# Stepping the RWKV recurrence by halves of two neighbouring pairs, with the centring products beside the steps

## The chip, the cores and the metric

The kernel runs on one core of one Trainium2 chip, alone. The metric is the device time of one launch in microseconds, the median of three runs.

## The reference

Two layers over 512 tokens and 2048 channels. Layer A is RWKV-7 time mixing: four 2048x2048 projections (receptance, keys, values, gates), two low-rank paths, a recurrence over time for 32 heads of 64 channels, an output projection and a LayerNorm. Layer B is differential attention over 8 heads with its own projections, an output projection and a LayerNorm. What the change touches is the recurrence:

```python
def step(S, inp):
    r_t, w_t, k_t, v_t, kk_t, a_t = inp
    sa = jnp.einsum('bhvk,bhk->bhv', S, kk_t)
    S = (S * w_t[:, :, None, :]
         - sa[..., None] * (kk_t * a_t)[:, :, None, :]
         + v_t[..., None] * k_t[:, :, None, :])
    y = jnp.einsum('bhvk,bhk->bhv', S, r_t)
    return S, y
...
mu = jnp.mean(y, -1, keepdims=True)
yc = y - mu
var = jnp.mean(yc * yc, -1, keepdims=True)
y = (yc * lax.rsqrt(var + GN_EPS)).reshape(B, T, C) * gn_g + gn_b
```

The kernel does it by chunks of 64 tokens: within a chunk everything is products with a prepared inverse, and only the state goes from chunk to chunk.

## The kernel before

**Dense products.** Each projection is 16 products (one per 128 output channels, 512 tokens wide). A product is 16 steps, and a step is three 128x512 matmuls into the PSUM tile `mm` (operands are split in two parts: `xh,whi`, then `xl,whi`, then `xh,wlo`). After each step `product` calls `fill.tick()`. A tick lets each waiting job (a Python generator) trace its next piece; `yield n` makes a job sit out n ticks. So between the three matmuls of one step and those of the next there is one place, called a **gap** below, where other matmuls can stand, and TensorE (`mm` keeps its program order) runs them there. A gap with nothing in it is a bare one.

**Pairs.** Two heads of 64 channels make a pair, 16 pairs in all. `phase1` prepares the operands of a pair during the key products and stores them in DRAM; `solve` (GpSimd) and `join` invert the triangular systems, still partly during the value products. From the third value product on, `phase2(p)` loads a pair again and makes its matrices, `chain(p)` steps through its 8 chunks, and `post(p)` normalises, in gaps of the value products and then of the gate products.

- `phase2(p)`, by fours of chunks: `K` times `AR` (128x128 products, `big<-AR,bdK`), masked by DVE into `LAR`; the **centring products** (`big<-cst,vt`, 16 of 128x64) whose result ACT copies into `W`; transposes of `K` (`big<-cst,bdK`); `X` times `R` (`big<-R,bdX`), copied into `Q` (`qs`). Loads: `R`, `AR` and `K` (`bdK`) come ahead (`load_r`, `load_ar`, `load_k`); `load_x` loads `bz`, `gls` and `X` (`bdX`). All these DMAs stand in one queue, SP's, in program order.
- `chain(p)`, per chunk: in one gap the two products `u<-W,LAR` (one per head, 128x64); ACT copies them into `W` (L829, L830); GpSimd makes `nl`, the decayed state (L836). In the next gap two products `u<-W,qs`, from which DVE makes the next chunk's state (L844, `W<-u,gls,nl`), and four products `y<-...` (128x64) for the output. So a chunk takes two gaps, a pair 16, and the pairs follow each other.
- `post(p)`: square, sum over a head (two 128x512 products, `onesr`), a reciprocal root on DVE, and the store `d_y`. `gates` loads `d_y` again, after gate product `GL`, when the recurrence's memory is given back.

TensorE gets 64-column products from `u`, `y` and the centring alone; the products of `K`, `X` and the transposes have 128 columns, like the dense ones. A call of one product of these small ones appears in the trace as two records.

Of the kernel before, what the change touches and what calls it, by code (L numbers as in the profile page):

```python
# [36 lines left out]
WL = 3                 # half blocks of weights in flight  # L37
# [6 lines left out]
# columns of the table of constants  # L44
# [4 lines left out]
# per-channel vectors, [128, NT] each  # L49
# [25 lines left out]
class Fill:  # L75
    """Jobs (generators) traced in steps between the dense products; a job yields the number of steps to sit out."""
# [22 lines left out]
def trunk(ctx, tc, xT, wts, vecs, wa1, wa2, lamb, subg, consts, outT):  # L99
# [44 lines left out]
    paired = [i * NT for i in (0, 1, 2, 3, 5, 9)]     # blocks multiplied together with the next one  # L144
    QT = 4                                              # k-tiles per split
# [57 lines left out]
    def products(xparts, n, begin, end, make=None, after=None):  # L203
        """n products; the first two, when paired, take turns so that each x part is needed less soon."""
# [30 lines left out]
    def rsqrt(src, pool, shape, tag, bufs=2, act=False):  # L235
        """q with RS_C * q = src ** -0.5: a seed from the exponent, then Newton's and Halley's steps."""
# [75 lines left out]
    # A transposed and the inverse X by 32 x 32 blocks: upper rows of A, its lower right block, X11, X21 and X22  # L312
# [19 lines left out]
    # ================= layer 1: RWKV-7 =================  # L332
# [19 lines left out]
    idle = p0.tile([P, T], F32, name="idle")      # products that only bring the tensor engine up to its clock  # L352
# [19 lines left out]
    def mm3(ps, a, b, start=True, stop=True):  # L372
        """Product of operands in two parts each."""
# [105 lines left out]
    def decay(p):  # L479
        """What pair p needs besides its keys."""  # L480
# [31 lines left out]
    def phase1(p, ks):  # L512
# [7 lines left out]
        # 1 / |kk| per head and token  # L520
# [94 lines left out]
    def join(g):  # L615
# [6 lines left out]
        def diagonal(dst, src):  # L622
            """The blocks of each two systems, on the diagonal."""
# [56 lines left out]
    def open_p2():  # L680
# [33 lines left out]
    def load_x(p):  # L714
# [3 lines left out]
        bz = p2.tile([P, T], F32, tag="bz", name="bz", bufs=1)  # L718
        gls = p2.tile([P, NCH], F32, tag="gls", name="gls", bufs=3)
        dma(bz, d_kz[p][:, T:2 * T])  # L720
# [6 lines left out]
        sts[p].update(bz=bz, gls=gls)  # L727
# [6 lines left out]
    def phase2(p):  # L734
        yield from until(("v", p), ("ar", p))
        if p >= 2:
            yield from until(("chain", p - 2))
        (R, AR), vt = lds.pop(p), vts.pop(p)
        st = sts[p] = {}
        fill.add(load_x(p), 1)  # L740
        K, X, Q = fixed["K"], fixed["X"], fixed[p % 2]
        LAR = p2.tile([P, 2, 2, NCH, L], F32, tag="LAR", name="LAR")
        W = p2.tile([P, 2, NCH, 2, L], F32, tag="W", name="W")
        for h, r in HEADS:
            dma(LAR[r, h], AR[r].rearrange("p w (c t) -> p w c t", t=L))
        G.memset(W[lo_, 0, 0, 0], 0.0)
        G.memset(W[hi_, 1, 0, 0], 0.0)
        more = p + 1 < NPAIR
        if more:
            fill.add(load_r(p + 1), 1)  # L750
        for q in range(2):
            cq = slice(q * 4, q * 4 + 4)
            pk = big()
            for i in range(4):
                c = q * 4 + i
                mm(pk[:, i * P:(i + 1) * P], lhsT=K[:, c, :], rhs=AR[:, :, c * L:(c + 1) * L], start=True, stop=True)
                if i == 1:
                    yield 1
            pkv = pk.rearrange("p (c two t) -> p c two t", two=2, t=L)
            for h, r in ((0, hi_), (1, lo_)):  # L760
                for w, msk in ((0, m_lt), (1, m_le)):
                    V.tensor_tensor(LAR[r, h, w, cq], pkv[r, :, w], over(msk[r], [L, 4, L]), ALU.mult)
            yield 1
        if more:
            fill.add(load_ar(p + 1), 9)
        # centred v by tokens
        pt = big()
        for c in range(NCH):
            cs = slice(c * L, (c + 1) * L)
            for h, r in ((0, hi_), (1, lo_)):  # L770
                mm(pt[r, cs], lhsT=vt[:, cs], rhs=cen[:, h * L:(h + 1) * L], start=True, stop=True)
            if c % 4 == 3:
                cq = slice(c - 3, c + 1)
                ptv = pt.rearrange("p (c o t) -> p c o t", t=L, o=1)[:, cq]
                S.copy(W[hi_, 0, cq], ptv[hi_].broadcast_to([L, 4, 2, L]))
                S.copy(W[lo_, 1, cq], ptv[lo_].broadcast_to([L, 4, 2, L]))
                yield 1
        for q in range(2):
            cq = slice(q * 4, q * 4 + 4)
            pt = big()  # L780
            for i in range(4):
                transpose(pt[:, i * P:(i + 1) * P], K[:, q * 4 + i, :], ident)
            ptv = pt.rearrange("p (c t) -> p c t", t=P)
            S.copy(Q[hi_, 0, cq, 0:L], ptv[hi_, :, 0:L])
            S.copy(Q[lo_, 1, cq, 0:L], ptv[lo_, :, L:P])
            yield 2
        if more:
            fill.add(load_k(p + 1), 3)
        yield from until(("ldx", p))
        for q in range(2):  # L790
            cq = slice(q * 4, q * 4 + 4)
            px = big()
            for i in range(4):
                c = q * 4 + i
                mm(px[:, i * P:(i + 1) * P], lhsT=X[:, c, :], rhs=R[:, c].rearrange("p a t -> p (a t)"), start=True, stop=True)
                if i == 1:
                    yield 1
            pxv = px.rearrange("p (c t) -> p c t", t=P)
            S.mul(Q[lo_, 0, cq], pxv[lo_], -1.0)
            S.mul(Q[hi_, 1, cq], pxv[hi_], -1.0)  # L800
            yield 1
        # bonus
        bv = p2.tile([P, T], F32, tag="bv", name="bv")
        V.tensor_mul(bv, vt, st["bz"])
        st.update(W=W, Q=Q, bv=bv, LAR=LAR)
        yield 1
        done.add(("p2", p))

    def phases2():
        yield 8  # L810
        for p in range(NPAIR):
            yield from phase2(p)

    def chains():
        for p in range(NPAIR):
            yield from until(("p2", p))
            yield from chain(p)
            fill.add(post(p), 1)

    def chain(p):  # L820
        st = sts[p]
        W, LAR, Q, gls = st["W"], st["LAR"], st["Q"], st["gls"]
        py = ps_y.tile([P, T], F32, tag="y", name="y")
        for c in range(NCH):
            pu = ps_u.tile([P, T], F32, tag="u", name="u")
            for h, r in HEADS:
                mm(pu[r, 0:L], lhsT=LAR[:, h, 0, c], rhs=W[:, h, c, 0], start=True, stop=True)
            with tc.high_priority():
                S.copy(W[lo_, 0, c, 1], pu[lo_, 0:L])  # L829
                S.copy(W[hi_, 1, c, 1], pu[hi_, 0:L])  # L830
            cs = slice(c * L, (c + 1) * L)
            gl = gls[:, c:c + 1]
            if c + 1 < NCH:
                nl = p2.tile([P, L], F32, tag="nl", name="nl")
# [475 lines left out]
```

## Time and profile before

| | us |
|---|---|
| runs | 2369.32, 2369.45, 2372.07; median 2369.45 |
| profiled execution, span from first to last instruction | 2371.4 |
| TensorE busy in it | 2281.1 (96%) |
| VectorE, ScalarE, GpSimd busy | 1371.7, 1085.0, 598.1 |
| mean granted TensorE clock | 0.983 |

The profiled execution has no time of its own beside its span; the span lies inside the range of the three runs and 1.95 us above their median. TensorE is the engine to look at. Its busy time is not its work, though: matmuls overlap, so a stretch in which each starts later than it could still counts as busy. What a gap costs is read from the starts of the matmuls in order of time.

### The profile page before, as it was taken

The numbers are of one execution on the slowest core, as the hardware profiler recorded it, in microseconds if no ns is written. First come the engines' busy times: TensorE is split into PE (matmuls) and PEld (weight loads), VectorE is DVE, ScalarE is ACT, GpSimd is POOL, SyncE is SP. The second block draws the span as 40 slices with busy tenths as digits, with TensorE's granted clock in tenths as the row PEclk, the third lists the DMA queues.
The fourth block names the chain that finished last, engine by engine and source line by source line (L and its number), as shares of the span: only waits on it lengthen the run. The fifth ranks groups of instructions, "written<-read, shape, count | busy, mean of one in ns | idle before, by whom it ended". The sixth has DMA issues, their size and how long they took to land.

```text
span 2371.4 us, 34536 instructions
## 1 busy us (share of the span) xinstructions
PE 2281.1 (96%) x12894; PEld 1822.3 (77%) x12894; DVE 1371.7 (58%) x2451; ACT 1085.0 (46%) x2228; POOL 598.1 (25%) x817
## 2 busy tenths in 40 slices
PE   8999999989999999999999989999999999999995
PEld 5887877777667776678888768888888888888884
DVE  7556887795566666764445465353453544536554
ACT  6556655564555556643333353343333433334223
POOL 4223052858563335720023240000000000000113
PEclk9999999989999999999999999999999999999997
DMA  6445555577546545533333312222222222222222
GB/s 213 143 136 178 169 190 177 170 222 213 135 126 162 150 132 146 153 102 135 116 107 120 116 62 89 89 80 89 89 81 96 80 91 81 89 89 80 98 90 88
DMA packets 195079, 294.93 MB, mean 124 GB/s; under 512 B 115296, under 2 KB 119648, under 8 KB 194912
## 3 DMA queue, kind: packets, MB, share of 16 engines
q10 hardware_dynamic: 45648, 166.22, 20.8%
q1 hardware_dynamic: 144144, 109.71, 16.3%
q0 software_dynamic: 5120, 16.81, 2.5%
q8 instruction: 101, 1.65, 0.3%
q14 instruction: 66, 0.54, 0.1%
HBM read 239.13 MB, written 45.15 MB: 120 GB/s over the span
## 4 chain that ended last, share of the span: by engine, by line
PE 79%; POOL 7%; DVE 4%; issue 3%; DMA 3%; ACT 2%; SPq 1%; POOLq 0%; ACTq 0%; DVEq 0%
PE mm L105 64%; PE big L105 6%; PE u L105 2%; POOL z L605 2%; POOL tm L603 2%; DMA xin<-in_xT 2%; PE s L105 1%; PE y L105 1%; PE o L105 1%; PE big L108 1%; POOL xm L269 1%; SPq L111 1%; PE t L108 1%; POOL xin L268 1%; DVE wlo L176 1%
## 5 line engine op out<-in xcount | busy, mean ns | idle before, releaser
L105 PE MATMUL mm<-xh,whi 128*128 128x512 f32 x2560 | 1043.6, 408 | 6.7 <-ACT xh L231 2.3
L105 PE MATMUL mm<-xl,whi 128*128 128x512 f32 x2560 | 1006.7, 393 | 11.5 <-DVE xl L232 6.6
L105 PE MATMUL mm<-xh,wlo 128*128 128x512 f32 x2560 | 1006.3, 393 | 5.7 <-DVE wlo L176 5.5
L176 DVE TENSOR_TENSOR wlo<-wraw,whi 128x512 fp32r<-128x512 f32 x640 | 474.5, 742 | 597.7 <-ACT whi L175 564.3
L175 ACT CAST whi<-wraw 128x512 fp32r<-128x512 f32 x640 | 396.9, 620 | 727.3 <-PE mm L105 712.7
L105 PEld LDWEIGHTS mm<-xh,wlo 128*128 128x128 f32 x2560 | 483.9, 189 | 112.3 <-DVE wlo L176 8.5
L105 PEld LDWEIGHTS mm<-xl,whi 128*128 128x128 f32 x2560 | 485.4, 190 | 105.2 <-DVE xl L232 10.6
L105 PEld LDWEIGHTS mm<-xh,whi 128*128 128x128 f32 x2560 | 484.7, 189 | 104.6 <-ACT xh L287 4.9
L1118 POOL TENSOR_SCALAR dist<-dist 128x512 f32<-128x512 f32 x8 | 12.4, 1546 | 654.6 <-DVE zz L1148 654.6
L836 POOL TENSOR_SCALAR nl<-W,gls 64x64 f32<-64x64 f32 x224 | 115.0, 513 | 158.6 <-DVE W L844 146.3
L844 DVE SCALAR_TENSOR_TENSOR W<-u,gls,nl 64x64 f32<-64x64 f32 x224 | 63.4, 283 | 91.8 <-PE u L105 70.5
L266 ACT ACTIVATE xm<-xin,omu 128x512 f32<-128x512 f32 x96 | 68.2, 721 | 46.3 <-DMA xin<-in_xT 36.8
L603 POOL TENSOR_TENSOR tm<-z,at 128x31 f32<-128x31 f32 (+15 forms) x124 | 81.1, 654 | 31.1 <-DMA at<-d_ad 22.8
L605 POOL TENSOR_TENSOR z<-z,tm 128x31 f32<-128x31 f32 (+15 forms) x124 | 85.9, 693 | 8.4
L969 POOL TENSOR_TENSOR lna<-lna,zt 128x512 f32<-128x512 f32 x26 | 42.6, 1639 | 170.0 <-DVE zt L1244 115.8
L268 POOL TENSOR_SCALAR xin<-xin,vec 128x512 f32<-128x512 f32 x54 | 48.7, 902 | 140.6 <-ACT xm L266 52.1
L269 POOL TENSOR_TENSOR xm<-xm,xin 128x512 f32<-128x512 f32 x54 | 81.8, 1517 | 3.5
L829 ACT COPY W<-u 64x64 f32<-64x64 f32 x128 | 26.3, 205 | 101.6 <-PE u L105 94.7
L105 PEld LDWEIGHTS u<-W,LAR 128*64 128x64 f32 x512 | 28.7, 135 | 55.5 <-DVE W L844 27.3
L1077 POOL TENSOR_TENSOR xin<-xin,lns 128x512 f32<-128x512 f32 x15 | 19.7, 1311 | 194.6 <-ACT lns L957 148.9
L1147 ACT ACTIVATE sc<-sc,mx 128x128 f32<-128x128 f32 (+3 forms) x64 | 35.9, 561 | 57.8 <-DVE mx L1145 57.8
L288 DVE TENSOR_TENSOR xl<-xm,xh 128x512 fp32r<-128x512 f32 x64 | 57.4, 909 | 6.4 <-ACT xh L287 5.6
(246 smaller groups left out, 2742.2 us busy)
## 6 DMA issues: line engine op xcount, KB each, us to landing
wraw<-in_w_in ACTq DMA_DIRECT2D x125, 512.0 KB, 3.7
wraw<-in_w_oa ACTq DMA_DIRECT2D x32, 512.0 KB, 3.6
wraw<-in_w_v ACTq DMA_DIRECT2D x32, 512.0 KB, 3.5
wraw<-in_w_k ACTq DMA_DIRECT2D x32, 512.0 KB, 3.4
wraw<-in_w_q ACTq DMA_DIRECT2D x32, 512.0 KB, 3.5
wraw<-in_w_g ACTq DMA_DIRECT2D x32, 512.0 KB, 3.5
wraw<-in_w_ob ACTq DMA_DIRECT2D x32, 512.0 KB, 3.5
xin<-in_xT POOLq DMA_DIRECT2D x48, 256.5 KB, 3.8
```

The lines of the kernel that those rows point to most:

```text
L105: tc.keep_in_program_order(nc.tensor.matmul(*args, **kw))
L108: tc.keep_in_program_order(nc.tensor.transpose(*args))
L175: S.copy(hi, raw)
L176: V.tensor_sub(lo, raw, hi.bitcast(F32))
L266: S.mul(t, xt[:, 1:T + 1], sc)
L268: G.tensor_scalar(xp, xp, mu, 0.0, ALU.mult, ALU.add)
L269: G.tensor_add(t, t, xp)
L288: V.tensor_sub(lo, raw, hi.bitcast(F32))
L603: G.tensor_tensor(tv, z[:, j:j + 1, 0:n].broadcast_to([P, ni, n]), at_[:, j, j + 1:H2].rearrange("p (i o) -> p i o", o=1).broadcast_to([P, ...
L605: G.tensor_tensor(z[:, j + 1:H2, 0:n], z[:, j + 1:H2, 0:n], tv, ALU.subtract)
L836: G.tensor_scalar(nl[r], W[r, h, c, 0], gl[r], 0.0, ALU.mult, ALU.add)
L844: V.scalar_tensor_tensor(W[r, h, c + 1, 0], pm_[r, 0:L], gl[r], nl[r], ALU.mult, ALU.add)
```

## The change

A pair's preparation is cut in two: `phase2(p)` becomes `half(p, 0)` and `half(p, 1)`, each for four chunks, with `LAR`, `W` and `Q` of half the size and four of each in place of two. A round of `chain` now steps two halves together: chunk i of `half(p, 0)` and chunk i of `half(p - 1, 1)`, in the same PSUM tile. Its first gap has four products `u<-W,LAR`, its second four `u<-W,qs` and eight `y`; between them `yield 2` leaves a gap out. There are 17 rounds of 4 chunks, 4 gaps each, in place of 16 of 8 chunks with 2. The centring products are not traced where `half` comes to them, but put in the list `cols`, and `run_cols` places them right ahead of the next `u` products. `load_ar` and `load_k` come later in a pair and `load_x` earlier relative to their use; `bz` is gone, its data is loaded into `bv`. The output is copied to `ys` by halves and squared from there. `GL` is 5.

```diff
-        for i in range(2):
-            fixed[i] = p2.tile([P, 2, NCH, P], F32, name=f"qs{i}", bufs=1)
+        for i in range(4):
+            fixed[i] = p2.tile([P, 2, HC, P], F32, name=f"qs{i}", bufs=1)
...
-        dma(bz, d_kz[p][:, T:2 * T])
...
+    HC = NCH // 2
+    cols = []
+    going = [False]
+
+    def run_cols():
+        while cols:
+            cols.pop(0)()
+
+    def half(p, q):
+
+        if q == 0:
+            yield from until(("v", p), ("ar", p))
+            sts[p] = dict(zip(("R", "AR"), lds.pop(p)), vt=vts.pop(p))
+            fill.add(load_x(p), 1)
+            if p + 1 < NPAIR:
+                fill.add(load_r(p + 1), 1)
...
+        n = 2 * p + q
+        if n >= 4:
+            yield from until(("ch", n - 4))
+        K, X, Q = fixed["K"], fixed["X"], fixed[n % 4]
+        LAR = p2.tile([P, 2, 2, HC, L], F32, tag="LAR", name="LAR", bufs=4)
+        W = p2.tile([P, 2, HC, 2, L], F32, tag="W", name="W", bufs=4)
...
+            dma(LAR[r, h], AR[r].rearrange("p w (c t) -> p w c t", t=L)[:, :, cq])
...
+        if q:
+
+            if p >= 3:
+                yield from until(("y", p - 3))
+            st["bv"] = p2.tile([P, T], F32, tag="bv", name="bv", bufs=3)
+            dma(st["bv"], d_kz[p][:, T:2 * T])
...
+        if q and p + 1 < NPAIR:
+            fill.add(load_ar(p + 1), 2)
+        yield 1
+
+        def centred():
+
+            pt = big()
+            for i in range(HC):
+                cs = slice((q * HC + i) * L, (q * HC + i + 1) * L)
+                for h, r in ((0, hi_), (1, lo_)):
+                    mm(pt[r, i * L:(i + 1) * L], lhsT=vt[:, cs], rhs=cen[:, h * L:(h + 1) * L], start=True, stop=True)
+            ptv = pt[:, 0:HC * L].rearrange("p (c o t) -> p c o t", t=L, o=1)
+            S.copy(W[hi_, 0], ptv[hi_].broadcast_to([L, HC, 2, L]))
+            S.copy(W[lo_, 1, :, 1], ptv[lo_, :, 0])
+            S.copy(W[lo_, 1, :, 0], ptv[lo_, :, 0])
+            done.add(("cen", p, q))
+
+        cols.append(centred)
...
+        if q and p + 1 < NPAIR:
+            fill.add(load_k(p + 1), 1)
+        yield 2
+        yield from until(("ldx", p))
...
+        if q:
+            V.tensor_mul(st["bv"], vt, st["bv"])
+            done.add(("vt", p))
...
+        for s in range(NPAIR + 1):
+            act = [(s - 1, 1)] * (s > 0) + [(s, 0)] * (s < NPAIR)
+            for p, q in act:
+                yield from until(("p2", p, q))
+            going[0] = True
+            yield from chain(act)
+            going[0] = False
+
+    def chain(act):
+        py = ps_y.tile([P, 2, HC * L], F32, tag="y", name="y")
+        for i in range(HC):
+            run_cols()
             pu = ps_u.tile([P, T], F32, tag="u", name="u")
...
+            for e, (p, q) in enumerate(act):
+                W, LAR, Q = sts[p][q]
+                for h, r in HEADS:
+                    mm(pu[r, e * L:(e + 1) * L], lhsT=LAR[:, h, 0, i], rhs=W[:, h, i, 0], start=True, stop=True)
...
+            yield 2
+            if i + 1 == HC and act[-1][1] == 0:
+                yield from until(("w", act[-1][0], 1))
+            run_cols()
+            pm_ = ps_u.tile([P, T], F32, tag="u", name="u")
...
-    GL = 4
+    GL = 5
```

**TensorE, a value product in the middle of the recurrence, before.** Every gap holds a step's products, and each is followed by the three dense ones:

```order
L105 MATMUL u<-W,LAR 64x64 x2
L105 MATMUL big<-AR,bdK 128x128 x2
L105 MATMUL mm<-xh,whi 128x512
L105 MATMUL mm<-xl,whi 128x512
L105 MATMUL mm<-xh,wlo 128x512
L105 MATMUL u<-W,qs_5827 64x64 x2
L105 MATMUL y<-LAR,W 64x64
L105 MATMUL y<-qs_5827,W 64x64
L105 MATMUL y<-LAR,W 64x64
L105 MATMUL y<-qs_5827,W 64x64
L105 MATMUL big<-AR,bdK 128x128 x2
```

The same place after, from the first gap of a product to the third:

```order
L105 MATMUL u<-W,LAR 64x64 x4
L105 MATMUL big<-AR,bdK 128x128 x2
L105 MATMUL mm<-xh,whi 128x512
L105 MATMUL mm<-xl,whi 128x512
L105 MATMUL mm<-xh,wlo 128x512
L105 MATMUL big<-AR,bdK 128x128 x2
L105 MATMUL mm<-xh,whi 128x512
L105 MATMUL mm<-xl,whi 128x512
L105 MATMUL mm<-xh,wlo 128x512
L105 MATMUL u<-W,qs_5827 64x64 x2
L105 MATMUL u<-W,qs_5829 64x64 x2
L105 MATMUL y<-LAR,W 64x64
```

The `u` products of two halves stand together now, and the gap between two steps of the recurrence holds 128-column products alone.

**VectorE, the same product, before:** the state (`W<-u,gls,nl`) of a step stands ahead of the masks (`LAR<-big,cst`).

```order
L804 TENSOR_TENSOR bv<-vt,bz 128x512
L176 TENSOR_TENSOR wlo<-wraw,whi 128x512
L864 TENSOR_TENSOR lo<-y_9259,hi 128x512
L844 SCALAR_TENSOR_TENSOR W<-u,gls,nl 64x64 x2
L762 TENSOR_TENSOR LAR<-big,cst 64x256 x4
L844 SCALAR_TENSOR_TENSOR W<-u,gls,nl 64x64 x2
```

After:

```order
L176 TENSOR_TENSOR wlo<-wraw,whi 128x512
L906 TENSOR_TENSOR lo<-y_9469,hi 128x512
L823 TENSOR_TENSOR bv<-vt,bv 128x512
L779 TENSOR_TENSOR LAR<-big,cst 64x256 x4
L878 SCALAR_TENSOR_TENSOR W<-u,gls,nl 64x64 x4
L176 TENSOR_TENSOR wlo<-wraw,whi 128x512
```

The multiplication by `bv`, whose operand is loaded in the same product now, and the masks stand between two states.

**SP's queue, one pair, before** (the rows of `join` between `R` and `AR` in some pairs are not in this one):

```order
L111 DMA LAR<-AR 64x1024 x2
L111 DMA bz<-d_kz_128 128x512
L111 DMA gls<-d_kz_128 128x8
L111 DMA bdX<-d_xu_162 32x8x32
L111 DMA bdX<-d_xl_166 32x8x64
L111 DMA bdX<-d_xu_162 32x8x32
L111 DMA bdX<-d_xl_166 32x8x64
L111 DMA R<-d_rb_145 128x1024
L111 DMA AR<-d_ar_113 128x1024
L111 DMA bdK<-d_kz_129 64x8x64 x2
```

After, from the second half of a pair on:

```order
L111 DMA LAR<-AR 64x2x256 x2
L111 DMA bv<-d_kz_128 128x512
L111 DMA AR<-d_ar_113 128x1024
L111 DMA bdK<-d_kz_129 64x8x64 x2
L111 DMA LAR<-AR 64x2x256 x2
L111 DMA gls<-d_kz_129 128x8
L111 DMA bdX<-d_xu_162 32x8x32
L111 DMA bdX<-d_xl_166 32x8x64
L111 DMA bdX<-d_xu_162 32x8x32
L111 DMA bdX<-d_xl_166 32x8x64
L111 DMA R<-d_rb_146 128x1024
```

The next pair's `AR` follows the copy of the second half at once, and its `LAR` copies and `X` loads follow that `AR`.

## Rows read from the trace of the kernel before

**Rows 1.** Page: span; busy time and share of TensorE.

```profile
span 2371.4 us, 34536 instructions
...
PE 2281.1 (96%) x12894; PEld 1822.3 (77%) x12894; DVE 1371.7 (58%) x2451; ACT 1085.0 (46%) x2228; POOL 598.1 (25%) x817
```

**Rows 2.** Stretches: length; busy of PE, PEld, DVE, ACT, POOL; PEclk, DMA share, GB/s.

```profile
720.90:913.70 192.80, 192.63 (x1916) 137.90 (x1914) 118.83 (x259) 109.62 (x279) 60.99 (x125) 1.00 0.56 148
913.70:1007.10 93.40, 84.65 (x739) 59.29 (x738) 73.43 (x128) 63.01 (x147) 69.97 (x93) 0.98 0.55 147
```

**Rows 3.** TensorE in order of time (start, duration): a bare gap between.

```profile
1100.06 0.39 PE L105 MATMUL mm<-xh,wlo 128*128 128x512 f32 x1
...
1100.73 0.39 PE L105 MATMUL mm<-xh,wlo 128*128 128x512 f32 x1
```

**Rows 4.** TensorE in order of time: two `u` products in one gap.

```profile
759.97 0.40 PE L105 MATMUL mm<-xh,wlo 128*128 128x512 f32 x1
760.30 0.34 PE L105 MATMUL u<-W,LAR 128*64 128x64 f32 x4
...
761.13 0.40 PE L105 MATMUL mm<-xh,wlo 128*128 128x512 f32 x1
```

**Rows 5.** TensorE in order of time: eight centring products in one gap.

```profile
574.26 0.40 PE L105 MATMUL mm<-xh,wlo 128*128 128x512 f32 x1
...
575.78 0.40 PE L105 MATMUL mm<-xh,wlo 128*128 128x512 f32 x1
```

**Rows 6.** TensorE in order of time: four `y` products in one gap.

```profile
788.80 0.40 PE L105 MATMUL mm<-xh,wlo 128*128 128x512 f32 x1
...
790.08 0.40 PE L105 MATMUL mm<-xh,wlo 128*128 128x512 f32 x1
```

**Rows 7.** TensorE in order of time: two `u` and four `y` products.

```profile
776.23 0.40 PE L105 MATMUL mm<-xh,wlo 128*128 128x512 f32 x1
...
777.67 0.40 PE L105 MATMUL mm<-xh,wlo 128*128 128x512 f32 x1
```

**Rows 8.** TensorE in order of time: two `u` and eight centring products.

```profile
770.58 0.40 PE L105 MATMUL mm<-xh,wlo 128*128 128x512 f32 x1
...
772.20 0.40 PE L105 MATMUL mm<-xh,wlo 128*128 128x512 f32 x1
```

**Rows 9.** TensorE in order of time: two `K` times `AR` products alone.

```profile
569.70 0.39 PE L105 MATMUL mm<-xh,wlo 128*128 128x512 f32 x1
...
570.84 0.39 PE L105 MATMUL mm<-xh,wlo 128*128 128x512 f32 x1
```

**Rows 10.** TensorE in order of time: two `u`, two `X` times `R`.

```profile
780.66 0.40 PE L105 MATMUL mm<-xh,wlo 128*128 128x512 f32 x1
...
782.26 0.40 PE L105 MATMUL mm<-xh,wlo 128*128 128x512 f32 x1
```

**Rows 11.** SP's queue in order of time, at the first pair.

```profile
570.49 1.15 SPq L111 DMA_DIRECT2D LAR<-AR  x2
...
575.08 0.45 SPq L111 DMA_DIRECT2D bdX<-d_xl  x1
```

**Rows 12.** Tile `bdX`, 690 to 900 us: from issue to landing.

```profile
DMA to landing us min/median/max: 2.0/2.5/6.1
```

**Rows 13.** Tile `bz`, 690 to 900 us: from issue to landing.

```profile
DMA to landing us min/median/max: 2.9/4.0/5.0
```

**Rows 14.** VectorE, 720.9 to 913.7 us: busy, mean ns, idle before.

```profile
L844 DVE SCALAR_TENSOR_TENSOR W<-u,gls,nl 64x64 f32<-64x64 f32 x98 | 27.8, 283 | 38.8 <-PE u L105 37.0
L762 DVE TENSOR_TENSOR LAR<-big,cst 64x256 f32<-64x256 f32 x56 | 21.2, 418 | 1.2 <-PE big L105 0.5
...
L804 DVE TENSOR_TENSOR bv<-vt,bz 128x512 f32<-128x512 f32 x7 | 4.8, 692 | 10.6 <-DMA d_y<-bv 10.5 <-DVE W L844 0.2
```

**Rows 15.** DMA issues, 720.9 to 913.7 us: KB each, median us to landing.

```profile
LAR<-AR SPq DMA_DIRECT2D x14, 256.0 KB, 3.9
...
AR<-d_ar SPq DMA_DIRECT2D x7, 512.0 KB, 4.7
```

More of the change, by code (lines that the diff above doesn't have):

```diff
@@ L726, in load_x @@
             dma(X[m_:(h + 1) * L, :, h * L:(h + 1) * L], d_xl[g][s0:s0 + NCH].rearrange("c i e -> i c e"))
-        sts[p].update(bz=bz, gls=gls)
+        sts[p].update(gls=gls)
         done.add(("ldx", p))
@@ L732, in start_loads @@
             fill.add(f(p), delay)
[L734 to L743, printed above, removed]
-        for h, r in HEADS:
[L745 to L762, printed above, removed]
-            yield 1
[L764 to L807, printed above, removed]
@@ L810, in phases2, with halves2 @@
+    def halves2():
         yield 8
         for p in range(NPAIR):
-            yield from phase2(p)
+            for q in range(2):
+                yield from half(p, q)
     def chains():
[L815 to L824, printed above, removed]
+        for s in range(NPAIR + 1):
[5 more added lines that the diff above has]
+            going[0] = False
@@ L825, in chain @@
+    def chain(act):
+        py = ps_y.tile([P, 2, HC * L], F32, tag="y", name="y")
+        for i in range(HC):
+            run_cols()
             pu = ps_u.tile([P, T], F32, tag="u", name="u")
-            for h, r in HEADS:
-                mm(pu[r, 0:L], lhsT=LAR[:, h, 0, c], rhs=W[:, h, c, 0], start=True, stop=True)
+            for e, (p, q) in enumerate(act):
+                W, LAR, Q = sts[p][q]
+                for h, r in HEADS:
+                    mm(pu[r, e * L:(e + 1) * L], lhsT=LAR[:, h, 0, i], rhs=W[:, h, i, 0], start=True, stop=True)
@@ L828, in chain @@
             with tc.high_priority():
[L829 to L834, printed above, removed]
-                for h, r in HEADS:
-                    G.tensor_scalar(nl[r], W[r, h, c, 0], gl[r], 0.0, ALU.mult, ALU.add)
-            yield 1
-            if c + 1 < NCH:
-                pm_ = ps_u.tile([P, T], F32, tag="u", name="u")
-                for h, r in HEADS:
-                    mm(pm_[r, 0:L], lhsT=Q[:, h, c, 0:L], rhs=W[:, h, c, 1], start=True, stop=True)
-                with tc.high_priority():
-                    for h, r in HEADS:
-                        V.scalar_tensor_tensor(W[r, h, c + 1, 0], pm_[r, 0:L], gl[r], nl[r], ALU.mult, ALU.add)
@@ L845, in chain @@
-            for h, r in HEADS:
-                mm(py[r, cs], lhsT=W[:, h, c, 0], rhs=LAR[:, h, 1, c], start=True, stop=False)
-                mm(py[r, cs], lhsT=W[:, h, c, 1], rhs=Q[:, h, c, L:P], start=False, stop=True)
-            yield 1
-        ys = p2.tile([P, T], F32, tag="ys", name="ys", bufs=1)
-        S.copy(ys, py)
-        st["ys"] = ys
-        y2 = p2.tile([P, T], F32, tag="y2", name="y2", bufs=1)
-        S.activation(y2, py, AF.Square)
-        st["y2"] = y2
-        done.add(("chain", p))
+                for e, (p, q) in enumerate(act):
+                    W = sts[p][q][0]
+                    for h, r in HEADS:
+                        S.copy(W[r, h, i, 1], pu[r, e * L:(e + 1) * L])
@@ new lines, in chain @@
+            nls = {}
+            go_on = [(e, p, q) for e, (p, q) in enumerate(act) if q == 0 or i + 1 < HC]
+            for e, p, q in go_on:
+                W, gl = sts[p][q][0], sts[p]["gls"][:, q * HC + i:q * HC + i + 1]
+                nl = nls[e] = p2.tile([P, L], F32, tag=f"nl{e}", name="nl", bufs=1)
+                for h, r in HEADS:
+                    G.tensor_scalar(nl[r], W[r, h, i, 0], gl[r], 0.0, ALU.mult, ALU.add)
+            yield 2
+            if i + 1 == HC and act[-1][1] == 0:
+                yield from until(("w", act[-1][0], 1))
@@ new lines, in chain @@
+            run_cols()
+            pm_ = ps_u.tile([P, T], F32, tag="u", name="u")
+            for e, p, q in go_on:
+                W, LAR, Q = sts[p][q]
+                for h, r in HEADS:
+                    mm(pm_[r, e * L:(e + 1) * L], lhsT=Q[:, h, i, 0:L], rhs=W[:, h, i, 1], start=True, stop=True)
+            with tc.high_priority():
+                for e, p, q in go_on:
+                    gl = sts[p]["gls"][:, q * HC + i:q * HC + i + 1]
+                    nxt, j = (sts[p][q][0], i + 1) if i + 1 < HC else (sts[p][1][0], 0)
+                    for h, r in HEADS:
+                        V.scalar_tensor_tensor(nxt[r, h, j, 0], pm_[r, e * L:(e + 1) * L], gl[r], nls[e][r], ALU.mult, ALU.add)
@@ new lines, in chain @@
+            cs = slice(i * L, (i + 1) * L)
+            for e, (p, q) in enumerate(act):
+                W, LAR, Q = sts[p][q]
+                for h, r in HEADS:
+                    mm(py[r, e, cs], lhsT=W[:, h, i, 0], rhs=LAR[:, h, 1, i], start=True, stop=False)
+                    mm(py[r, e, cs], lhsT=W[:, h, i, 1], rhs=Q[:, h, i, L:P], start=False, stop=True)
+            yield 2
+        for e, (p, q) in enumerate(act):
+            st = sts[p]
+            if q == 0:
+                if p >= 2:
+                    yield from until(("y", p - 2))
+                st["ys"] = p2.tile([P, T], F32, tag="ys", name="ys", bufs=2)
+            S.copy(st["ys"][:, q * HC * L:(q + 1) * HC * L], py[:, e])
+            done.add(("ch", 2 * p + q))
+            if q:
+                fill.add(post(p), 1)
@@ L857, in post @@
     def post(p):
         st = sts.pop(p)
-        ys, y2, bv = st["ys"], st["y2"], st["bv"]
+        ys, bv = st["ys"], st["bv"]
+        y2 = p2.tile([P, T], F32, tag="y2", name="y2", bufs=1)
+        S.activation(y2, ys, AF.Square)
         yield 1
@@ L884, in begin_v @@
             fill.add(chains())
-            fill.add(phases2())
+            fill.add(halves2())
     def end_v(p, ps):
+        while p >= 3 and ("vt", p - 3) not in done:
+            fill.tick()
         vts[p] = pm.tile([P, T], F32, tag="vt", name="vt", bufs=3)
```

45 lines of the change are left out of this document (40 added, 5 removed).

## The prediction

> **What bounds the kernel now.** The page's first rows give TensorE 96% of the span, no other engine over 58% [rows 1]. That says where to look, not what can be gained, since a busy TensorE may be starting late. So I read next the busy times by stretch. In seven value products of the recurrence, 192.8 us, TensorE shows 192.6 us busy at a granted clock of 1.00, VectorE 118.8, ScalarE 109.6, GpSimd 61.0; in the following gate products, 93.4 us, TensorE shows 84.7 and VectorE and GpSimd over 70 each [rows 2]. So the first stretch is set by TensorE's own order, and in the second others come near it. Third I read TensorE in order of time, for the price of a gap: from the start of a step's last matmul (`mm<-xh,wlo`) to the start of the next step's. A bare gap's step takes .67 us; I use .68 [rows 3]. What is above that is what the gap holds.
>
> **What a gap costs.** Two `u` products: 1.16 us, so .48 [rows 4]. Eight centring products: 1.52, .84 [rows 5]. Four `y`: 1.28, .60 [rows 6]. `u` and `y` together: 1.44, .76, not 1.08 [rows 7]. `u` and centring together: 1.62, .94, not 1.32 [rows 8]. So a gap with 64-column products costs something for being visited, and then little for each product. With a visit v and a product e, 2e + v = .48 and 8e + v = .84 give e = .06, v = .36. It predicts .60 for four (measured .60), .72 for six (.76) and .96 for ten (.94). For 128-column products there is no such visit: two of `AR` and `K` alone cost .46 [rows 9], and two of `R` and `X` add .92 - .48 = .44 to a gap with `u` [rows 10].
>
> **Term 1, visits removed.** TensorE does the same products before and after; only their gaps differ. Counted in the order from the middle of the third value product to the third gate product, 258 gaps hold 64-column products before and 137 after; in a steady product 16 and 8. That is 121 x .36 = **-43.6 us**. Bounds: v is .32 from the pair `u` and `y` (.48 + .60 - .76) and .38 from `u` and centring (.48 + .84 - .94), so -38.7 to -46.0.
>
> There is a smaller price to be read. Entering the gap with `u` takes 760.30 - 759.97 = .33 us [rows 4], a bare matmul .67 / 3 = .22 [rows 3]; if only this .11 were saved by a visit, the sum would be 121 x .11 = -13. [...] The trace disagrees with that as the whole price: merged gaps show .32 to .38 saved [rows 4 to 8].
>
> **Term 2, the start.** The first pair's centring products no longer stand between its masks and its `R` times `X`. TensorE reaches `X` sooner: from 569.70 [rows 9], three gaps of 1.14 and a bare one, at 573.8. The last load of `bdX` is issued at 575.08 [rows 11], some .7 sooner without the issue of `bz` (.72), at 574.4, and lands 2.5 later, 6.1 at most [rows 12]: 576.9, or 580.5. The wait is 3.1 to 6.7 us; I take **+4**, nearer to the median.
>
> **Term 3, VectorE held by `bv`.** In the new order `bv<-vt,bv` stands ahead of the masks and the states, and its operand is loaded only when SP comes to the second half. Behind it on VectorE wait four masks and four states; for the states waits TensorE's next `u`. The copies of `LAR` before it are issued in 1.15 us [rows 11] once the last `y` of the round before is done; then comes the load, which lands 4.0 later (2.9 to 5.0, `bz`'s load being the same transfer) [rows 13]. The last `y` lies about 1.05 ahead of the product's first gap (a bare step and the end of the one before), so the operand is there 4.1 us after that gap begins. Then VectorE needs .69 + 4 x .42 + 4 x .28 = 3.5 [rows 14]: the state is ready at 7.6. TensorE comes to the `u` of the fifth gap after four steps of .68, a first gap of .36 + 4 x .06 + .46, a second of .46, a third of .36 + 12 x .06 + .46 and an empty one: 5.8, and the centring products in front take .36 + 8 x .06 = .8: 6.6. It waits 1.0 to 1.1 us. Ten pairs have this order, so **+11 us**; with the bounds of the landing 0 to +21.
>
> **Term 4, the gate products.** In 913.7 to 1007.1 us TensorE is idle 93.4 - 84.7 = 8.8 us by its own record, and VectorE and GpSimd have 73.4 and 70.0 us of work [rows 2]. Three products lose 3 x 8 x .36 = 8.6 us of visits; 93.4 - 8.8 - 8.6 = 76 is close to VectorE's 73.4, so the visits saved are not all kept. I take **+3**, bounds 0 and +8.6.
>
> **Terms of nothing.** The copies `ys` by halves, two more copies of `W` from centring and squaring from SBUF lie on ScalarE, with 109.6 of 192.8 us busy; two `nl` for one on GpSimd, with 61.0 [rows 2]. `LAR` is copied by four DMAs in place of two, each of half the size, by a queue whose engines are 56% busy [rows 2]. A step of the recurrence has a gap free between its parts, so the copies into `W` have the 1.14 us of a step with two 128-column products [rows 9], or more, where they had one gap too. `GL` moves the gates' late part by one product, work that TensorE does either way. If ScalarE or GpSimd were late, TensorE's next `u` would wait, once per step of a round: .1 us each would be 68 x 2 x .1 = 14 us; nothing in rows 2 points there.
>
> **Sum.** -43.6 + 4 + 11 + 3 = -25.6. The profiled execution spans 2371.4 us [rows 1], so 2345.8 there; it lies 1.95 above the median of the runs, so 2369.45 - 25.6 = **2344 us**.
>
> **Rivals.** A is this forecast, with 2334 to 2356 for its own bounds.
>
> B: every wait is covered. For it speaks that a wait of 1 us is small against what the landings vary by (2.9 to 5.0 [rows 13]); against it the order on VectorE. 2369.45 - 43.6 = 2326.
>
> C: a visit costs only the entry, .11 us, as the merged gaps might be cheap because of overlap with what stands around them: -13 + 18 = 2374. For it the .33 of [rows 4], against it [rows 7, 8].
>
> D, the slower side: SP's loop of loads becomes the bound. A pair's last `LAR` copies must land (3.9) before the next `AR` may overwrite, `AR` lands in 4.7 [rows 15], then follow two copies 1.15, `gls` 1.00, four loads of `bdX` about 2.0 by their issue times [rows 11], and the last landing 2.5 [rows 12]: 15.3 us. `R` times `X` of the next half stands in the eleventh gap, about 16.8 us into a product. So 1.5 us are left, and what exceeds them is paid in each of 14 pairs, as the loop closes on itself. It is slower than before from 25.6 / 14 = 1.8 us beyond, that is landings 3.3 us longer in all than the medians. With `bdX` landing in its longest 6.1 [rows 12], and the other two each 1 us late as `bz` can be [rows 13], it is 5.6 - 1.5 = 4.1 per pair: 2344 + 57 = 2401 us. Against it: those are the longest, and all three at once.
>
> **How the numbers follow.** A .59, B .15, C .08, D .10, and .08 for waits that I have not found and that eat the gain in part. The likeliest is 2344. The range, 2326 to 2364, takes in A and B whole and the nearer part of the rest; C and D beyond it hold about 2 in 10. Within .2%, 4.7 us, is about what a measurement of this kernel cannot tell from no change. Faster: A, B and half of the unfound waits, with a little of C: .80. Slower: D and half of C: .12. The same: .08.
>
> **What the new profile should show.** The seven products of [rows 2] take 192.8 - 7 x 8 x .36 + 7 x 1.1 = 180 us. A gap with four `u` alone costs .36 + 4 x .06 = .60, with four `u` and eight `y` 1.08. TensorE waits for VectorE's state (`W`) about 1 us in each steady product's fifth gap, and once some 4 us for `bdX` near 574 us; nothing for `AR` or `bdK`. Before 569 us and after the recurrence nothing changes but the shift. The prediction is wrong if gaps with 12 products cost 1.3 us or more, if `bdX` is waited for in every pair, or if VectorE's and ScalarE's turns with twice the states at once make TensorE wait at every step.

## The result, and the profile after

The changed kernel takes 2349.45 us (median of four runs, 2347.14 to 2350.59), against 2370.04 for the kernel before: ratio .9907, interval .9893 to .9921. That is 20.6 us less, where 25.6 were forecast; a second measurement of the same kernel, beside its own runs of the kernel before, gave .9901 (.9884 to .9917). One of its four executions took 4431.6 us and is not counted.

The page of the changed kernel, its span and the first row of the engines, which answer to [rows 1]:

```profile
span 2347.5 us, 34688 instructions
...
PE 2240.8 (95%) x12894; PEld 1821.5 (78%) x12894; DVE 1366.7 (58%) x2451; ACT 1083.6 (46%) x2276; POOL 594.8 (25%) x819
```

TensorE executes as many instructions as before and is busy 40 us less: a visit was counted as busy. The profiled execution is 23.9 us shorter than that of before, more than the medians are apart. The time of this execution lies 2.0 us above its span (2349.5 and 2347.5). By that, an estimate, that of before, with a span of 2371.4, lay above the median of its runs by some 3 us, and not by the 1.95 that comes of setting its span against their times. What follows goes by the profiles.

The seven products of [rows 2] and the three after them, in the changed kernel (length; busy of PE, PEld, DVE, ACT, POOL; PEclk, DMA share, GB/s):

```profile
718.99:893.11 174.12, 173.99 (x1915) 136.54 (x1914) 118.70 (x259) 106.29 (x297) 59.15 (x122) 1.00 0.62 161
893.11:985.27 92.16, 78.22 (x739) 60.97 (x738) 72.85 (x130) 66.79 (x160) 70.12 (x97) 0.96 0.55 154
```

The first stretch fell from 192.8 to 174.1 us, and TensorE is idle in .1 us of it. The second fell from 93.4 to 92.2 only, though it lost 24 visits too; TensorE's busy time fell by 6.4 us there and its idle time grew from 8.8 to 13.9. Cut at the same products in both traces (at the last matmul of a product's first step), the change over the whole program is:

| stretch (products) | before, us | after | change | visits fewer x .36 | taken back |
|---|---|---|---|---|---|
| up to the recurrence | 563.4 | 563.9 | +.5 | 0 | .5 |
| 34 to 39 (start, inversion) | 158.9 | 155.1 | -3.8 | 33: 11.9 | 8.1 |
| 40 to 46 (steady) | 192.8 | 174.1 | -18.7 | 56: 20.2 | 1.5 |
| 47 to 49 (mixing for the gates) | 93.5 | 92.2 | -1.3 | 24: 8.6 | 7.3 |
| 50 and later | rest | rest | -.6 | 8: 2.9 | 2.3 |

The products are counted through the program, 32 to 47 for the values and 48 and on for the gates. Taken back is what the saved visits should have given and did not. The second row, in the kernel before and in the changed one:

```profile
563.42:722.32 158.90, 153.67 (x1413) 111.35 (x1412) 86.23 (x178) 78.30 (x195) 98.82 (x190) 0.99 0.60 155
563.88:718.99 155.11, 142.40 (x1395) 110.34 (x1394) 82.38 (x170) 76.71 (x209) 97.53 (x191) 0.97 0.60 152
```

Prices, from TensorE in order of time in the changed kernel (the start of a step's last matmul to the next one's): four `u` products and their eight `y` with four transposes, then the empty gap; and further on four `u` alone.

```profile
747.40 0.40 PE L105 MATMUL mm<-xh,wlo 128*128 128x512 f32 x1
...
749.57 0.39 PE L105 MATMUL mm<-xh,wlo 128*128 128x512 f32 x1
...
750.27 0.40 PE L105 MATMUL mm<-xh,wlo 128*128 128x512 f32 x1
...
765.01 0.40 PE L105 MATMUL mm<-xh,wlo 128*128 128x512 f32 x1
...
766.29 0.40 PE L105 MATMUL mm<-xh,wlo 128*128 128x512 f32 x1
```

Four `u` cost 1.28 - .68 = .60, as .36 + 4 x .06 says. The gap with twelve products and the transposes costs 2.17 - .68 = 1.49, where 1.54 was reckoned.

The fifth gap of the product that begins at 769.35 us, where the third term stands (SP's issue, VectorE, TensorE):

```profile
769.27 0.56 SPq L111 DMA_DIRECT2D bv<-d_kz  x1
...
772.20 0.69 DVE L823 TENSOR_TENSOR bv<-vt,bv 128x512 f32<-128x512 f32 x1 [0.59 <-DMA bv<-d_kz]
...
772.91 1.53 DVE L779 TENSOR_TENSOR LAR<-big,cst 64x256 f32<-64x256 f32 x4
...
774.36 1.22 DVE L878 SCALAR_TENSOR_TENSOR W<-u,gls,nl 64x64 f32<-64x64 f32 x4
...
775.93 0.29 PE L105 MATMUL u<-W,LAR 128*64 128x64 f32 x4
```

The order is the forecast one, `bv`, masks, states. But the states end at 774.36 + 1.22 = 775.58, and the `u` begins at 775.93 behind its centring products: nothing is waited for. The load of `bv` from 700 to 893 us:

```profile
DMA to landing us min/median/max: 2.0/2.9/4.5
```

Waits of TensorE at the first pairs, 560 to 700 us (in all, times, longest):

```profile
PE u L105 <- DVE W L878: 7.8, 4, 5.7
PE big L105 <- DMA bdX<-d_xl: 1.9, 1, 1.9
PE big L105 <- DMA bdK<-d_kz: 1.8, 2, 1.3
```

The 5.7 us wait in it, in order of time on VectorE and TensorE, with the granted clock of the stretch behind it:

```profile
685.49 1.03 DVE L608 COPY zt<-z 64x1024 f32<-64x1024 f32 x1 [5.50 <-POOL z L605]
...
687.16 1.22 DVE L878 SCALAR_TENSOR_TENSOR W<-u,gls,nl 64x64 f32<-64x64 f32 x4
...
687.48 1.42 PE L105 MATMUL u<-W,LAR 128*64 128x64 f32 x8 [5.75 <-DVE W L878]
...
689.85 0.63 PE L105 MATMUL mm<-xh,wlo 128*128 128x512 f32 x1
...
691.13 0.63 PE L105 MATMUL mm<-xh,wlo 128*128 128x512 f32 x1
```

```profile
678.00:692.00 14.00, 8.25 (x73) 6.34 (x72) 7.40 (x13) 4.69 (x13) 8.53 (x18) 0.78 0.12 43
```

VectorE stood at `zt` till GpSimd's inversion was done, and the states stood behind it. After the wait a bare step takes 1.28 us, not .68.

The last value product, where the mixing for the gates begins, which makes their input from tiles of `xin` by `xm` on ScalarE and two operations on GpSimd (ScalarE, then TensorE), and ScalarE's largest wait from 893 to 985 us:

```profile
895.33 0.72 ACT L266 ACTIVATE xm<-xin,omu 128x512 f32<-128x512 f32 x1 [4.67 <-DMA xin<-in_xT]
...
899.77 0.91 ACT L856 COPY W<-u 64x64 f32<-64x64 f32 x4
...
900.04 0.96 PE L105 MATMUL u<-W,qs 128*64 128x64 f32 x7 [3.68 <-ACT W L856]
```

```profile
ACT xm L266 <- DMA xin<-in_xT: 11.5, 6, 4.7
```

ScalarE waits for a tile of `xin`, with the copies of `u` some operations behind it, and TensorE for those copies. TensorE's waits for them in these three products, in the kernel before and in the changed one:

```profile
PE u L105 <- ACT W L829: 4.1, 4, 2.4
...
PE u L105 <- ACT W L856: 9.0, 4, 3.7
```

### The profile page after: what moved, and what is told of

It reads as the page before. It is cut to its first block, busy times and chain, and to the rows that moved or that the text cites. A ratio compares the mean times of both kernels' runs of the same rounds, so it can differ in the third digit from the quotient of the medians.

```text
span 2347.5 us, 34688 instructions
## 1 busy us (share of the span) xinstructions
PE 2240.8 (95%) x12894; PEld 1821.5 (78%) x12894; DVE 1366.7 (58%) x2451; ACT 1083.6 (46%) x2276; POOL 594.8 (25%) x819
## 4 chain that ended last, share of the span: by engine, by line
PE 65%; POOL 4%; DVE 3%; DMA 1%; issue 1%; ACT 1%; POOLq 0%; SPq 0%; DVEq 0%
PE mm L105 55%; PE big L105 3%; PE s L105 1%; PE u L105 1%; PE o L105 1%; PE y L105 1%; POOL z L605 1%; POOL tm L603 1%; POOL nl L863 1%; DMA xin<-in_xT 1%; PE t L108 1%; POOL zt L1086 1%; PE big L108 0%; PE st L105 0%; DVE xl L232 0%
## 5 line engine op out<-in xcount | busy, mean ns | idle before, releaser
L863 POOL TENSOR_SCALAR nl<-W,gls 64x64 f32<-64x64 f32 x224 | 105.5, 471 | 157.9 <-DVE W L878 143.0
L114 POOL DMA_DIRECT2D xin<-in_xT x64 | 36.3, 567 | 169.0 <-issue 131.8
L856 ACT COPY W<-u 64x64 f32<-64x64 f32 x256 | 53.1, 207 | 33.2 <-DVE wlo L176 14.5
L288 DVE TENSOR_TENSOR xl<-xm,xh 128x512 fp32r<-128x512 f32 x64 | 57.2, 905 | 11.5 <-ACT xh L287 10.6
L271 DVE SCALAR_TENSOR_TENSOR xm<-xin,vec,xm 128x512 f32<-128x512 f32 x42 | 34.3, 821 | 29.9 <-ACT xm L266 29.9
```

The costliest lines, as they stand in the source:

```text
L288: V.tensor_sub(lo, raw, hi.bitcast(F32))
L856: S.copy(W[r, h, i, 1], pu[r, e * L:(e + 1) * L])
L863: G.tensor_scalar(nl[r], W[r, h, i, 0], gl[r], 0.0, ALU.mult, ALU.add)
```

## The experiments

All start from the changed kernel. Ratios are to the kernel before on the same chip; .9901 to .9907 is no difference from the changed kernel.

**The price of a visit.** `y_apart`: the `y` products one gap behind their `u`.

```diff
+            yield 1
             cs = slice(i * L, (i + 1) * L)
...
-            yield 2
+            yield 1
```

> The changed kernel, with the y products one gap behind the u products of their step. TensorE does the same products; by its order 204 gaps hold 64-column products instead of 137. If a visit costs .36 us whatever stands in it, this is 67 x .36 = 24 us slower than the changed kernel (21 to 25 with the bounds .32 and .38): about 2373 us, nearly all of the gain lost again. If only the entry of a gap costs, .11 us, it is 7 us: 2357 us. If the gain came from steps that now have a free gap between them, and not from visits, nothing is lost: 2349 us.

Measured: 2357.8 us, .9941 (.9924 to .9958): 8 to 10 us slower, not 24. The total comes near the 7 us of the cheaper price, but the trace says otherwise. The same two gaps as above, `u` with transposes and then the eight `y`:

```profile
748.90 0.40 PE L105 MATMUL mm<-xh,wlo 128*128 128x512 f32 x1
...
750.56 0.40 PE L105 MATMUL mm<-xh,wlo 128*128 128x512 f32 x1
...
752.12 0.40 PE L105 MATMUL mm<-xh,wlo 128*128 128x512 f32 x1
```

They take 1.66 + 1.56 = 3.22 us, where together they took 2.17 + .70 = 2.87: .35 for one visit, at the granted clock 1.00 of both stretches. By stretches:

```profile
720.00:901.30 181.30, 181.30 (x1916) 136.06 (x1914) 117.14 (x258) 107.61 (x297) 63.80 (x123) 1.00 0.58 156
901.30:993.00 91.70, 81.94 (x740) 60.33 (x738) 69.39 (x130) 66.62 (x160) 71.09 (x97) 0.96 0.53 150
```

The steady seven grew by 7.2 us for 28 visits, .26 each; a steady product without waits grew from 24.82 to 26.02 us for four, .30 each. The three with the mixing did not grow at all (91.7 against 92.2), with 12 visits more. Where TensorE sets the pace a visit costs .30 to .35, a little less than was reckoned, and in the products with the mixing, where it waits anyway, nothing. That is where my 24 us failed.

**The list of centring products.** `centring_in_place`:

```diff
-        cols.append(centred)
+        centred()
```

> The changed kernel, with the centring products traced where half comes to them instead of being kept for the next u products. By TensorE's order 141 gaps hold 64-column products instead of 137, the four more all in the first two pairs, since later a half comes to its centring in a gap that has u products anyway. Visit theory: 4 x .36 = 1.4 us slower, and the wait for bdX at the start (1.9 us) mostly gone: no difference, 2347 to 2351 us. Rival: the list is a part of the gain by itself (centring at once also moves its copies on ScalarE), then 10 us or more slower.

Measured: 2344.4 us, .9887 (.9872 to .9902): by its median some 4 us faster than the changed kernel, with intervals that overlap. The list is no part of the gain.

**GL.** `gl4`:

```diff
-    GL = 5
+    GL = 4
```

> The changed kernel with GL = 4 as before. The last output is stored during the gate product 4 (the fifth), so at its beginning the program waits for it without dense products between: of the last pair's normalising some 12 us of work on VectorE, ScalarE and in the store's landing stand uncovered. Expected 8 to 12 us slower than the changed kernel, 2357 to 2361 us. Rival, as the prediction had it: GL only moves work, no difference, 2347 to 2351 us.

Measured: 2352.5 us, .9918 (.9904 to .9933), some 3 us slower by the median, intervals overlapping. The place is as expected and the size not. TensorE in `gl4`:

```profile
1023.98 0.50 PE L105 MATMUL big<-hi,onesr 128*128 128x512 f32 x1 [1.78 <-ACT hi L905]
...
1025.03 0.79 PE L105 MATMUL big<-lo,onesr 128*128 128x512 f32 x1 [0.54 <-DVE lo L906]
...
1026.47 0.63 PE L105 MATMUL mm<-xh,wlo 128*128 128x512 f32 x1
...
1027.75 0.63 PE L105 MATMUL mm<-xh,wlo 128*128 128x512 f32 x1
```

Only the two sums of the last pair are waited for; what follows them on VectorE and in the store has nothing of TensorE's behind it. The gate product with that wait takes 20.2 us, 4.0 longer than the same one in the changed kernel: the two waits are 2.3 of it, and a bare step behind them takes 1.28 us (1026.47 to 1027.75).

**`bv`.** First `bv_late`, which moves the load behind the first two `K` times `AR` products in the program:

```diff
         for i in range(HC):
...
             if i == 1:
                 yield 1
+            if i == 1 and q:
...
+                dma(st["bv"], d_kz[p][:, T:2 * T])
```

> The changed kernel, with the load of bv issued one gap later; VectorE's order stays (the multiplication by bv ahead of masks and states). In the trace of the changed kernel bv lands 2.9 us after issue (not the 4.0 that the prediction took from bz), and in the product at 769 us the states end .3 us ahead of the u products of the fifth gap (775.58 and 775.87). If that chain is what sets the fifth gap once it is late, one gap more, 1.1 us, makes TensorE wait .8 us in each of some ten pairs: 8 us slower, 2355 to 2359 us. Rival: something else covers it, no difference (2347 to 2351 us).

Measured: 2348.3 us, .9901 (.9886 to .9916). This told nothing: SP did not wait for TensorE, and issued the load right behind the copies of `LAR` as before, ahead of the first gap's `u` (770.69 and 771.10 us in the eleventh product). Then `bv_behind_ar`, which puts it behind a load that SP issues later (that of `AR`, at 773.37 us in `bv_late`):

```diff
+    def load_bv(p):
...
+        dma(sts[p]["bv"], d_kz[p][:, T:2 * T])
...
         if q and p + 1 < NPAIR:
             fill.add(load_ar(p + 1), 2)
+        if q:
+            fill.add(load_bv(p), 2)
```

> The changed kernel, with the load of bv behind that of the next AR in SP's queue. VectorE's order changes with it: bv<-vt,bv now stands behind the masks and the states, so no state waits for it. By the prediction's third term (1.1 us in each of ten pairs) this is 11 us faster, 2337 us. By the trace of the changed kernel, where bv lands after 2.9 us and the states end .3 us before they are needed, only the pairs with a late landing (4.5 us: 1.0 us of wait) gain: 1 to 2 us, no difference that can be measured, 2345 to 2349 us, with the products from 700 to 890 us as long as before.

Measured: 2347.5 us, .9893 (.9879 to .9908). The seven products:

```profile
716.00:888.50 172.50, 172.50 (x1916) 135.73 (x1914) 118.55 (x259) 106.14 (x297) 56.01 (x122) 1.00 0.62 163
```

With no state behind `bv` at all they gain 1.6 us (1.2 against `after_again` below), not 7 x 1.1.

**One kernel twice.** `after_again` is the changed kernel.

> The changed kernel unaltered, to be compared with the others on the same chip: .990 to .992 of the kernel before, as the first time; its profile shows how far the waits of two executions of one kernel differ (43.9 us of late gaps by the first).

Measured: 2348.1 us, .9901. Its seven steady products take 173.7 us (174.1 before), the three mixing ones 93.3 (92.2); 35 to 39 differ by 2 us. So stretches with waits differed by 1 to 2 us between these two executions.

**The waits that took visits back.** `zt_pool`:

```diff
-        V.tensor_copy(zt[NSYS:P], z[NSYS:P].rearrange("p i c -> p c i"))
+        G.tensor_copy(zt[NSYS:P], z[NSYS:P].rearrange("p i c -> p c i"))
```

> The changed kernel, with the copy zt<-z (L608) on GpSimd, behind the inversion that makes z, instead of on VectorE. In the changed kernel's trace TensorE waits 5.75 us for a state (W, L878) at 681 us; VectorE stands at zt<-z meanwhile, 5.50 us, till GpSimd is done with z, and the states are behind it. Theory: without zt there the states wait for nl alone (done at 683.64 instead of 687.16 less 1.03), so some 3 us of the wait go, and with them the slow steps after it (two of 1.28 instead of .68): 3 to 4.5 us faster, 2345 to 2347 us. Rival: GpSimd, busy with the inversion, delays nl by as much or the next wait takes the time over: no difference.

Measured: 2336.6 us, .9851 (.9834 to .9867): 11.5 us faster than `after_again` on the same chip, more than expected and mostly elsewhere. In the products 37 to 39 only 1.5 us went against `after_again`; the gap with the long wait is late by 3.1 us instead of 7.3, and others grew. Some 7 us came out of one key product at 350 us, where another `zt` stands in VectorE's queue: TensorE waits there for ScalarE's `rb`, and `rb` for `nry`, which VectorE makes behind `zt`. Waits at that place in the changed kernel, then in `zt_pool`:

```profile
PE big L108 <- ACT rb L528: 7.2, 1, 7.2
...
ACT rb L528 <- DVE nry L253: 4.5, 1, 4.5
...
DVE zt L608 <- POOL z L605: 4.2, 1, 4.2
```

```profile
PE big L108 <- ACT rb L528: 2.2, 1, 2.2
```

The kernel before has the same `zt` wait there, so this gain isn't the change's; it wasn't tried on that kernel.

`xin_early`:

```diff
+        if p == 10:
+            while len(xg.x) < 3:
+                xg.x.append(x_tile(len(xg.x)))
```

> The changed kernel, with the first three loads of xin for the gates' mixing issued at the beginning of the eleventh value product and not in the last. In the trace ScalarE waits 4.67 us for xin at 895 us, with six operations and the copies of u behind it, and TensorE 3.68 us for those copies (5.5 us with the slow step after it). Theory: that wait goes, and little else: 4 to 6 us faster, 2343 to 2346 us. Rival: ScalarE and GpSimd have too much mixing in these products, whenever it is loaded, and the same time is waited a little later: no difference.

Measured: 2347.2 us, .9896 (.9882 to .9911), no difference. The wait moved with the load (`xin_early`, ScalarE and TensorE in the eleventh product):

```profile
769.99 0.72 ACT L266 ACTIVATE xm<-xin,omu 128x512 f32<-128x512 f32 x1 [4.41 <-DMA xin<-in_xT]
...
773.92 0.89 ACT L856 COPY W<-u 64x64 f32<-64x64 f32 x4
...
774.18 0.96 PE L105 MATMUL u<-W,qs 128*64 128x64 f32 x7 [2.81 <-ACT W L856]
```

That product takes 28.4 us instead of 23.5, and the three with the mixing 86.5 instead of 92.2. By these waits it is the place of `xm` in ScalarE's order, just ahead of the copies, that costs the time, and not when the load is issued; an order with `xm` elsewhere was not tried.

`nl_act`:

```diff
-                    G.tensor_scalar(nl[r], W[r, h, i, 0], gl[r], 0.0, ALU.mult, ALU.add)
+                    S.mul(nl[r], W[r, h, i, 0], gl[r])
```

> The changed kernel, with the decayed state nl on ScalarE (64x64, like its copies of u, .22 us each) instead of GpSimd (.47 each). Theory: the waits between 640 and 690 us and some of those from 893 to 990 us come from nl having to take turns with the inversion and the mixing on GpSimd, which hold up nl, the loads of xin issued behind nl, and so TensorE: 6 to 14 us faster, 2335 to 2343 us, with the steady products unchanged at 24.8 us. Rival: ScalarE, on whose copies of u every step depends, gets .9 us more of work per step; if the copies of u come behind it, 68 steps are later by up to .5 us each and the steady product grows by 1 to 2 us: 15 us slower.

Measured: 2344.6 us, .9888 (.9873 to .9902), some 4 us faster by the median, overlapping. Both theories held, in different places. The seven steady products take 180.9 us instead of 174.1. Products 35 to 39 take 132.5 instead of 134 to 136, and the gain that outweighs the loss lies in the three with the mixing, 86.2 instead of 92.2:

```profile
713.40:894.30 180.90, 177.82 (x1916) 138.91 (x1914) 119.92 (x259) 143.72 (x404) 17.90 (x33) 0.99 0.59 162
894.27:980.43 86.16, 79.50 (x740) 61.74 (x738) 72.63 (x130) 75.91 (x192) 36.68 (x43) 0.93 0.52 150
```

So by this one execution some 6 us of what those three products lose lie in GpSimd's turns between `nl` and the mixing.

`no_mix`:

```diff
+            if self.i == 3:
+                self.parts.append(xv_.parts[m])
+                return
```

> The changed kernel without the mixing for the gates: the gate products take the values' operands, so their input is not the reference's and sixteen loads of xin, with what ScalarE, GpSimd and VectorE make of them, are left out. If this mixing is what takes back the saved visits from the last value product on, the four products from 893 to 1008 us (114.6 us) go to the 24.8 us of a steady one, with the last at about 21: 95 us, so 17 to 19 us faster, 2330 us. Rival: the waits there are the recurrence's own (two states at a time on VectorE, GpSimd's nl, the end of the rounds): at most 5 us faster.

Measured: 2325.7 us, .9805 (.9791 to .982). The seven products and the three after them:

```profile
719.50:894.20 174.70, 174.19 (x1915) 136.65 (x1915) 118.40 (x259) 107.35 (x301) 57.81 (x122) 1.00 0.60 160
894.20:965.40 71.20, 70.65 (x740) 55.46 (x738) 51.32 (x114) 45.31 (x125) 18.61 (x49) 1.00 0.52 142
```

The steady stretch is as it was, and the three products go from 92.2 to 71.2 us, 23.7 each. The kernel before was not run without the mixing, but both traces hold one product with the same work for TensorE and no mixing, the eleventh of the values:

```profile
777.67:804.16 26.49, 26.49 (x247) 18.76 (x246) 16.95 (x38) 15.22 (x39) 7.88 (x17) 1.00 0.48 138
769.35:792.81 23.46, 23.46 (x248) 18.51 (x246) 17.07 (x37) 14.99 (x43) 10.02 (x18) 1.00 0.61 160
```

By it three such products would take 79.5 us before and 70.4 after, an estimate; with the mixing they took 93.5 and 92.2. So the visits do give 9 us, and the mixing's price, 14 us before and 21 to 22 after, takes most of them back.

**Combinations.** `zt_cen` has the edits of `zt_pool` and `centring_in_place`, `zt_cen_mix` this one besides:

```diff
-            raw = mix(self.x[m], self.i, m, (m > 1 and m % 2, m % 3 == 2, m % 3 > 0, True)[self.i])
+            raw = mix(self.x[m], self.i, m, (m > 1 and m % 2, m % 3 == 2, m % 3 > 0, m % 2)[self.i])
```

> The changed kernel with zt<-z on GpSimd and the centring products in place, both of which were faster alone (.9851 and .9887 of the kernel before, where the changed kernel is .9901). If the two gains are apart (products 24 and 37 to 39 the one, 47 to 50 the other), .984, 2332 us; if they take the same waits, no better than zt_pool, 2336 us.

> As zt_cen, with every second tile of the gates' mixing on VectorE (one operation of .74 us) instead of GpSimd (two, 2.2 us). If GpSimd's turns are what hold up nl and the loads of xin from 893 to 1008 us, 4 to 6 us faster than zt_cen, 2327 us. Rival: VectorE, with 73 us of work in such a stretch of 93, then holds up the states instead: no faster, or some us slower.

Measured: 2339.4 us, .9863 (.9847 to .988), and 2339.7, .9864 (.9847 to .988). Neither adds to `zt_pool`, and half of the mixing on VectorE changes nothing that can be measured. By its median the fastest kernel with the reference's whole work is `zt_pool`, .9851.

## Why the prediction was right

The time lies in the range and near the forecast. The price of a visit, which makes the whole gain, was right. That the sum of the waits came out right too is luck: the largest of them was not there, and others that I had at nothing or too small took its place.

**Term 1 held, in its price.** A steady product without waits went from 27.67 to 24.82 us for eight visits: 2.85 / 8 = .36. If each gap is set against the shortest gap of the same content, the gaps of the recurrence are late by 25.8 us in all before and 43.9 after; 23.9 + 18.1 = 42 us of TensorE's time was saved, where 43.6 was summed. Rival C's price, .11, falls with `y_apart` (.30 to .35). What makes up the price of a visit no run here shows.

**Term 2, +4 for the start, came near by luck.** The trace shows 1.9 us for `bdX`, below the bound of 3.1, and 1.8 for `bdK`, which I had said would not be waited for.

**Term 3, +11, is the one that failed.** The order on VectorE and the time of the `u` were right (6.6 reckoned after the product's first gap begins; 775.93 - 769.35 = 6.6). The landing was mis-sized: 4.0 from `bz` [rows 13], 2.9 measured for the same bytes, so the states are ready .3 us before they are needed. The forecast's lower bound, a landing of 2.9, was the case. The seven steady products, forecast at 180 us, took 174.1. `bv_behind_ar` shows what was left of the term in them, under 2 us.

**Term 4, +3, was mis-sized the other way.** In 47 to 49 the visits gave 1.3 of 8.6 us (nothing in `after_again`); 7.3 was taken back. I had asked whether VectorE's 73 us of work would fit in 76 us. They are not what binds: `no_mix` shows that the mixing costs 21 us there, and TensorE's longest waits (9.0 us, 4.1 before) run over ScalarE, which stands at `xm` for a tile of `xin` (11.5 us in six waits) with the copies of `u` behind it. By `nl_act` some 6 us of that lie in GpSimd's turns. Why moving half of the mixing to VectorE doesn't help stays open; so does what of the 21 us the loads alone are, and why the price is higher with two halves in a step.

**A loss that I had at nothing.** In 34 to 39 the visits gave 3.8 of 11.9 us. Besides the start it is the end of the inversion: VectorE waits at `zt` with the states behind it. In the steady products, with a free gap per step, no state is late by its own work (from 700 to 890 us no wait of TensorE shows), but at `zt` VectorE's queue stood still for 5.50 us, and the gap with twelve products and the transposes holds 1.49.

**GL, a term of nothing,** is worth 3 to 4 us: with `GL` 4 the last pair's sums stand open.

So 18 us of waits were forecast and 18 measured, but 11 of the forecast ones were not there, and as many others were. Rival B (every wait covered) held in the steady products alone, and rival D (SP's loop) didn't come about: TensorE waits for no load there.

## What to carry to other kernels

Price a gap by differences between gaps of different content in one trace: the visit here (.36 us) and the product (.06) came out of six rows and held in the changed kernel. Then ask of each stretch who sets its pace: of 121 visits removed, those in the steady stretch gave nearly all of their price, and those beside the inversion and the mixing a third or less. A latency taken from the same transfer among other neighbours is a guess (4.0 us for `bz`, 2.9 for `bv`), and a term that hangs on it wants a wide bound. And look for the waits in the queues of the engines that a recurrence passes through: here VectorE's 5.50 us at `zt` stood ahead of a wait of 5.75 us on TensorE, and ScalarE's 4.67 us at `xm` ahead of one of 3.68.

## What was not expected of the hardware

Behind the 5.75 us wait of TensorE at 681 us a bare step takes 1.28 us and not .68, and the clock granted to it is .50, where the steady products have 1.00. Behind the wait of 3.68 us at 896 us the clock granted from 901.30 to 904.00 us is .50 as well, and behind one of 2.29 us at 951 us, from 953.25 to 955.00, it is 1.00.

```profile
689.85:691.13 1.28, 1.28 (x4) 0.99 (x3) 1.24 (x2) 0.28 (x2) 0.68 (x1) 0.50 0.00 0
```

The step of 1.28 us in `gl4` stands behind two waits of 1.78 and .54. A bare step of 1.28 us costs .60 us on top of the wait. The prediction had no term for it. By the granted clocks of the two stretches with waits, .97 and .96 after against .99 and .98 before, 155.1 x .03 + 92.2 x .04 = 8 us of full clock are missing after and 158.9 x .01 + 93.5 x .02 = 3 before: an estimate, by which up to 5 of the 18 us that were taken back are the clock's.
